# One added product with 64 stationary columns, in the seven-product pairs and in the channel products of a two-layer trunk kernel

## The chip, the cores and the metric

The kernel runs on one core of one Trainium2 chip. The metric is the device time of one execution in microseconds. Three runs of the kernel before are given, and one more execution was profiled.

## The reference

Two layers, each with four phases that add to the residual `h` (512 tokens of 1024 values): a feed-forward half step, a mixer of three head groups, a cross attention to 256 memory tokens, and a second feed-forward half step. The feed-forward, which takes most of the time, is

```python
def swiglu_ffn(x, w_up, w_down):
    gate, up = jnp.split(x @ w_up, 2, axis=-1)
    return (jax.nn.silu(gate) * up) @ w_down
...
    h = h + 0.5 * rms_norm(ff, g[FFN1_POST])
```

with `x` 512 x 1024, `w_up` 1024 x 5632 and `w_down` 2816 x 1024, in float32. It occurs four times (two layers, two half steps).

## The kernel before

**Parts of a product.** Every weight and every activation is split in two parts, hi and lo (`whi`, `wlo`, `xhi`, `xlo`), and a product of the reference is three products on TensorE (hi hi, hi lo, lo hi), each of the type fp32r. ScalarE makes the hi part of a weight, VectorE the lo part, from the raw weights (`wraw`) that SP's queue loads.

**The upward product.** The input's transposed form lies in `xhi`, `xlo` as eight blocks of 128 channels by 512 tokens. The first channel blocks of a phase are done by `chans`, in two halves of 256 tokens: for the first `nj` outputs (4) a bank of PSUM is held, the first half of the tokens is multiplied for all of them, then the second half; that lets the work begin when two of the four token tiles are normalised. Further outputs take all 512 tokens at once. A product of `chans` writes a tile `ch`. The transposes that bring the next token tiles in (`tp<-ident,xn`, four to a group) stand between the products of `chans`.

**Seven products.** From the fourth pair of hidden blocks on (`SEVEN = range(3, NF)`, 19 pairs to an upward stretch, two outputs of 128 to a pair) an output block is made by seven products of half size instead of eight (`products`). They use sums of input blocks made once a phase (`form`) and sums of weight blocks made for each pair (`sums`). In the trace they write tiles `p`. Each of the seven is 4 channel blocks times 3 parts, so 12 TensorE products with 128 stationary columns and 256 moving ones, and a pair is 84. The seven run in the order P1 (weights `a`), P6 (`c`), P2 (`d`), P7 (`c`), P5 (`b`), P3 (`b`), P4 (`a`). VectorE joins their results (`w`), ScalarE applies the silu (`sg`).

**Order.** The streams (loads, splits, products, normalisation) are generators; a modelled clock picks the one that can start first and so fixes the order in which each engine's instructions are written. Nothing is reordered on the chip except by what waits.

Of the kernel before, what the change touches and what calls it, by code (L numbers as in the profile page):

```python
# [69 lines left out]
SEVEN = range(3, NF)  # L70
# [196 lines left out]
class Weave:  # L267
# [455 lines left out]
    def chans(self, n, nj, sink, over=None):  # L723

        held = []
        for half in range(2):
            for t in range(2):
                yield ("x", self.phase, 2 * half + t)
            for i in range(nj):
                if not half:  # L730
                    yield {"cur": 1}
                    held.append(self.bank("ch", True))
                    u = yield from self.unit(self.n(i))
                u = self.u[self.n(i)]
                yield from self.chan(held[i], u, 256 * half, 256 * half + 256, i == 0)
                if half:
                    self.spent(self.n(i))
                    sink(i, held[i])
        for i in range(nj, n):
            if self.n(i) in self.seven:  # L740
                yield from self.products(i)
            if self.n(i) in self.seven or self.n(i - 1) in self.seven:
                continue
            u = yield from self.unit(self.n(i))
            yield {"cur": 1}
            ps = self.bank("ch", True)
            yield from self.chan(ps, u, 0, S)
            self.spent(self.n(i))
            sink(i, ps)
        if over is not None:  # L750
            over()

    def products(self, i):

        k = self.k
        f, i = i // 2, self.n(i)
        yield ("forms",)

        def x(kh, th):
            return tuple(q[:, 4 * kh:4 * kh + 4, 256 * th:256 * th + 256] for q in (k.xhi, k.xlo))

        def prod(out, u, h, x, first=True, last=True):
            for kk in range(4):
                if kk % 2 == 0:
                    yield "T"
                k.mm3(out, tuple(q[:, 4 * h:4 * h + 4] for q in u), kk, (x[0][:, kk], x[1][:, kk]), first and kk == 0, last and kk == 3)

        lo, hi = slice(0, 256), slice(256, 512)  # L770
        s1, s2, s3, s4 = self.sx

        def bank(name):
            ps = self.bank(name, True)
            banks[name] = ps
            return ps

        banks = {}
        a = yield from self.unit((i, "a"))
        yield {"cur": 1}  # L780
        ps = bank("p17")
        self.spawn(self.combine(f, banks), 2 * f)
        yield from prod(ps[:, lo], a, 0, x(0, 0))
        self.fire(("P1", f))
        c = yield from self.unit((i, "c"))
        yield {"cur": 1}
        p2 = bank("p62")
        yield from prod(p2[:, lo], c, 1, s2)
        self.given(f, 2, 3)
        d = yield from self.unit((i, "d"))  # L790
        yield from prod(p2[:, hi], d, 0, x(1, 0))
        self.fire(("P2", f))
        self.spent((i, "d"))
        yield from prod(ps[:, hi], c, 0, s3)
        self.fire(("P7", f))
        self.given(f, 4, 5)
        self.spent((i, "c"))
        b = yield from self.unit((i, "b"))
        yield {"cur": 1}
        yield from prod(bank("p5")[:, lo], b, 0, s1)  # L800
        self.given(f, 0, 1)
        self.fire(("p5", f))
        yield {"cur": 1}
        ps = bank("p34")
        yield from prod(ps[:, hi], b, 1, x(1, 1))
        self.spent((i, "b"))
        yield from prod(ps[:, lo], a, 1, s4)
        self.fire(("p4", f))
        self.spent((i, "a"))
        if f == SEVEN[-1]:  # L810
            self.fire(("sevens",))

    def given(self, f, *tiles):

        if f == SEVEN[-1]:
            tiles = [j for j in tiles if self.phase or j < 4]
            self.hs_free.extend(tiles)
            self.free(hs=len(tiles))
# [1595 lines left out]
```

## Time and profile before

| | |
|---|---|
| three runs | 2329.0, 2330.9, 2335.39 us, median 2330.9 |
| the profiled execution | 2327.65 us, span of its instructions 2325.9 us |
| TensorE products | 15128, busy 99% of the span |
| VectorE / ScalarE / GpSimd busy | 79% / 50% / 12% |
| HBM | 138 GB/s over the span |

Products on TensorE are pipelined: the next one starts before the last has ended, so that the engine reads as busy throughout, and the time that one product costs is the distance from its start to the start of the next. That distance is called the pace below.

### The profile page before, as it was taken

The page shows a single profiled execution, that of the slowest core. Times are in us where ns is not written, and L with a number is a line of the kernel's source. Part 1 is how long each engine was busy: PE and PEld are TensorE (multiplying, and loading weights), DVE is VectorE, ACT ScalarE, POOL GpSimd, SP SyncE. Part 2 cuts the span into 40 slices and gives each one's busy share as a digit, 9 for nine tenths or more (in the row PEclk, how much of TensorE's full clock was granted, in tenths as well). Part 3 has the DMA queues.
Part 4 walks back from the last instruction along what each step waited for, and adds up shares of the span by engine and source line. Part 5 has one row for each costly group of instructions (what it writes and reads, how often), then busy time and mean ns, then how long its engine had stood idle before and what let it go on. Part 6 is the DMA issues. An engine that isn't in the chain of part 4 may idle for free.

```text
span 2325.9 us, 39137 instructions
## 1 busy us (share of the span) xinstructions
PE 2292.5 (99%) x15128; PEld 2066.8 (89%) x15128; DVE 1833.0 (79%) x2746; ACT 1155.4 (50%) x1963; POOL 290.0 (12%) x406
## 2 busy tenths in 40 slices
PE   9999999998999999999999999999999999999998
PEld 8999889887888899998899998897878888999987
DVE  7999777887766689996789996778876666999865
ACT  4444555544554454445544445545345545544554
POOL 2000011444200100000000000032442101000000
PEclk9999999999999999999999999999999999999999
DMA  5333676323555343336633336643236544333464
GB/s 166 105 105 110 218 218 179 89 71 93 192 207 181 110 127 109 106 112 192 180 110 109 109 112 197 194 107 95 61 121 210 182 166 133 103 108 110 126 200 145
DMA packets 323441, 323.72 MB, mean 139 GB/s; under 512 B 29507, under 2 KB 264501, under 8 KB 323254
## 3 DMA queue, kind: packets, MB, share of 16 engines
q1 hardware_dynamic: 323254, 321.21, 45.1%
q8 instruction: 119, 1.95, 0.3%
q14 instruction: 68, 0.56, 0.1%
HBM read 301.50 MB, written 19.66 MB: 138 GB/s over the span
## 4 chain that ended last, share of the span: by engine, by line
PE 92%; DVE 3%; ACT 2%; issue 1%; POOL 1%; DMA 0%; SPq 0%; DVEq 0%; POOLq 0%; ACTq 0%
PE p L141 32%; PE dn L141 27%; PE ch L141 14%; PE tk L141 4%; PE kv L141 4%; PE tp L141 1%; PE xs L141 1%; PE xo L141 1%; PE mo L141 1%; PE iy L141 1%; ACT whi L141 1%; PE iu L141 1%; POOL ss L141 1%; PE py L141 1%; PE mp L141 1%
## 5 line engine op out<-in xcount | busy, mean ns | idle before, releaser
L141 DVE TENSOR_TENSOR wlo<-wraw,whi 128x1024 fp32r<-128x1024 f32 (+2 forms) x491 | 564.1, 1149 | 180.6 <-ACT whi L141 179.8
L141 ACT ACTIVATE whi<-wraw 128x1024 fp32r<-128x1024 f32 (+2 forms) x492 | 481.8, 980 | 223.8 <-PE dn L141 134.3
L141 PE MATMUL p<-form,whi 128*128 128x256 f32 x2432 | 440.3, 281 | 0.0
L141 PE MATMUL dn<-whi,hs 128*128 128x512 f32 x1376 | 379.1, 391 | 0.0
L141 PEld LDWEIGHTS p<-form,whi 128*128 128x128 f32 x2432 | 376.2, 190 | 1.0
L141 PE MATMUL p<-form,wlo 128*128 128x256 f32 x1216 | 341.8, 281 | 0.0
L141 ACT ACTIVATE whi<-sums 128x1024 fp32r<-128x1024 f32 x152 | 161.2, 1063 | 309.8 <-DVE sums L141 223.8
L141 PEld LDWEIGHTS dn<-whi,hs 128*128 128x128 f32 x1376 | 255.4, 188 | 50.9
L141 PE MATMUL p<-xhi,whi 128*128 128x256 f32 x912 | 256.3, 281 | 0.0
L141 PE MATMUL p<-xhi,wlo 128*128 128x256 f32 x912 | 256.3, 281 | 0.0
L141 PE MATMUL p<-xlo,whi 128*128 128x256 f32 x912 | 256.3, 281 | 0.0
L141 PEld LDWEIGHTS p<-form,wlo 128*128 128x128 f32 x1216 | 228.3, 188 | 0.0
L141 PE MATMUL ch<-xhi,whi 128*128 128x256 f32 (+1 forms) x688 | 217.6, 323 | 0.2
L141 DVE TENSOR_TENSOR wlo<-sums,whi 128x1024 fp32r<-128x1024 f32 x152 | 185.0, 1219 | 38.5 <-ACT whi L141 38.5
L141 PE MATMUL dn<-wlo,hs 128*128 128x512 f32 x688 | 214.3, 390 | 0.0
L141 PE MATMUL ch<-xhi,wlo 128*128 128x256 f32 (+1 forms) x688 | 214.0, 318 | 0.2
L141 POOL TENSOR_SCALAR ss<-ss 128x1 f32<-128x1 f32 (+1 forms) x80 | 41.3, 516 | 1369.9 <-ACT jk L141 1232.5
L141 PE MATMUL ch<-xlo,whi 128*128 128x256 f32 (+1 forms) x688 | 202.2, 317 | 0.0
L141 DVE TENSOR_TENSOR w<-p,w 128x512 f32<-128x512 f32 (+1 forms) x304 | 187.3, 616 | 5.7 <-PE p L141 5.6
L141 PEld LDWEIGHTS p<-xlo,whi 128*128 128x128 f32 x912 | 175.1, 192 | 0.4
L141 PEld LDWEIGHTS p<-xhi,whi 128*128 128x128 f32 x912 | 171.2, 188 | 0.5
L141 PEld LDWEIGHTS p<-xhi,wlo 128*128 128x128 f32 x912 | 171.2, 188 | 0.0
(373 smaller groups left out, 4182.3 us busy)
## 6 DMA issues: line engine op xcount, KB each, us to landing
wraw<-in_ffn_w_down_dram SPq DMA_DIRECT2D x172, 512.0 KB
wraw<-in_ffn_w_up_dram SPq DMA_DIRECT2D x304, 256.0 KB
wraw<-in_w_in_dram SPq DMA_DIRECT2D x32, 512.0 KB
wraw<-in_xa_w_kv_dram SPq DMA_DIRECT2D x32, 512.0 KB
wraw<-in_w_out_dram SPq DMA_DIRECT2D x30, 512.0 KB
wraw<-in_xa_w_o_dram SPq DMA_DIRECT2D x30, 512.0 KB
wraw<-in_ffn_w_up_dram SPq DMA_DIRECT2D x24, 512.0 KB
xkv<-kvs SPq DMA_DIRECT2D x32, 256.0 KB
```

The lines of the kernel that those rows point to most:

```text
L141: return f(*args, **kw)
```

## The change

A method `pace` issues one TensorE product with 64 stationary columns (half of the 128) and 256 moving ones, into the first 64 partitions of a bank that the next product overwrites. It is called in two places: in `products`, in the first pair of each upward stretch only, between P1 and P6; and in `chans`, before the second output (`i == 1`) of the first token half. Nothing is removed.

```diff
@@ chans
                     u = yield from self.unit(self.n(i))
+                    if i == 1:
+                        yield "T"
+                        self.pace(held[i], u)
                 u = self.u[self.n(i)]
...
@@ products
         p2 = bank("p62")
+        if f == SEVEN[0]:
+            yield "T"
+            self.pace(p2, c)
         yield from prod(p2[:, lo], c, 1, s2)
...
+    def pace(self, ps, w):
+
+
+        self.T.matmul(ps[:64, :256], w[0][:, 0, :64], self.k.xhi[:, 0, :256], start=True, stop=True)
```

TensorE's order around the first pair of the first upward stretch, in the changed kernel (a row is a product, output tile, moving and stationary operand, partitions by moving columns; `p_653` is the bank of P1, `p_672` that of P6 and P2):

```order
256 L141 MATMUL p_653<-xhi,whi 128x256
257 L141 MATMUL p_653<-xlo,whi 128x256
258 L141 MATMUL p_653<-xhi,wlo 128x256
259 L141 MATMUL p_672<-xhi,whi 64x256
260 L141 MATMUL p_672<-form,whi 128x256 x2
261 L141 MATMUL p_672<-form,wlo 128x256
262 L141 MATMUL p_672<-form,whi 128x256 x2
```

One row came in, between the 12 products of P1 and the 12 of P6; there are four such rows in the program, one for each upward stretch.

TensorE's order in the last phase of the first layer (second feed-forward), at the end of the first output of `chans`, changed kernel first, where `tp` is a group of four transposes:

```order
3350 L141 MATMUL ch<-xlo,whi 128x256 x4
3351 L141 MATMUL ch<-xhi,whi 64x256
3352 L141 MATMUL ch<-xhi,whi 128x256
3353 L141 MATMUL ch<-xlo,whi 128x256
3354 L141 MATMUL ch<-xhi,wlo 128x256
3355 L141 MATMUL ch<-xhi,whi 128x256
3356 L141 MATMUL ch<-xlo,whi 128x256
3357 L141 MATMUL ch<-xhi,wlo 128x256
3358 L141 MATMUL tp<-ident,xn 128x128 x4
```

And the same place before:

```order
3350 L141 MATMUL ch<-xhi,wlo 128x256
3351 L141 MATMUL ch<-xhi,whi 128x256
3352 L141 MATMUL ch<-xlo,whi 128x256
3353 L141 MATMUL ch<-xhi,wlo 128x256
3354 L141 MATMUL ch<-xhi,whi 128x256
3355 L141 MATMUL ch<-xlo,whi 128x256
3356 L141 MATMUL ch<-xhi,wlo 128x256
3357 L141 MATMUL tp<-ident,xn 128x128 x4
```

The added product stands behind the first output's 24 products, and the modelled clock now writes the first group of transposes 6 products earlier: 30 products of `chans` stand ahead of it instead of 36. There are eight such added rows, one for each phase, and a group of transposes moves 6 products forward in five of the phases.

## Rows read from the trace of the kernel before

**Rows 1.** The page: busy time by engine; costliest groups (busy us, mean ns).
```profile
PE 2292.5 (99%) x15128; PEld 2066.8 (89%) x15128; DVE 1833.0 (79%) x2746; ACT 1155.4 (50%) x1963; POOL 290.0 (12%) x406
...
L141 PE MATMUL p<-form,whi 128*128 128x256 f32 x2432 | 440.3, 281 | 0.0
```

**Rows 2.** Windows: busy us (count) by engine, granted clock, DMA share, GB/s.
```profile
52.48:236.80 184.32, 184.32 (x1566) 184.31 (x1565) 171.23 (x224) 83.62 (x114) 0.00 (x0) 1.00 0.37 107
...
2011.52:2195.73 184.21, 184.21 (x1566) 184.21 (x1564) 171.41 (x223) 83.82 (x115) 0.00 (x0) 1.00 0.37 108
...
1989.85:2000.50 10.65, 10.65 (x95) 10.65 (x95) 10.55 (x11) 6.73 (x8) 0.00 (x0) 1.00 0.18 51
```

**Rows 3.** Timeline, PE, where the first upward stretch begins: start us, us.
```profile
52.26 0.39 PE L141 MATMUL ch<-xhi,wlo 128*128 128x512 f32 x1
52.48 0.28 PE L141 MATMUL p<-xhi,whi 128*128 128x256 f32 x1
...
53.19 0.28 PE L141 MATMUL p<-xhi,whi 128*128 128x256 f32 x1
```

**Rows 4.** Timeline, PE, products with 64 stationary columns within the mixer.
```profile
562.44 0.28 PE L141 MATMUL kv<-wraw,wlo 128*128 128x256 f32 x1
562.64 0.43 PE L141 MATMUL mo<-pair,gt 128*64 128x128 f32 x2
563.01 0.50 PE L141 MATMUL kv<-wraw,whi 128*128 128x256 f32 x2
563.35 0.28 PE L141 MATMUL kv<-wraw,wlo 128*128 128x256 f32 x1
```

**Rows 5.** Timeline, PE, behind four products of 64 rows by 64 columns.
```profile
611.49 0.41 PE L141 MATMUL it<-ident,pair 64*64 64x64 f32 x4
...
612.52 0.28 PE L141 MATMUL kv<-mch,wlo 128*128 128x256 f32 x1
...
613.20 0.28 PE L141 MATMUL kv<-mch,wlo 128*128 128x256 f32 x1
```

**Rows 6.** Timeline, PE, behind a wait in the channel products of a later phase.
```profile
838.86 0.28 PE L141 MATMUL ch<-xhi,whi 128*128 128x256 f32 x1
...
839.21 0.28 PE L141 MATMUL ch<-xhi,wlo 128*128 128x256 f32 x1
```

**Rows 7.** Timeline, PE, behind one product with 114 stationary rows and moving columns.
```profile
27.33 0.26 PE L141 MATMUL psp<-ident,prow 114*128 114x114 f32 x1
...
27.56 0.28 PE L141 MATMUL ch<-xlo,whi 128*128 128x256 f32 x1
...
28.15 0.28 PE L141 MATMUL ch<-xhi,whi 128*128 128x256 f32 x1
```

**Rows 8.** Timeline, PE, the attention scores `xs` behind a fast channel stretch.
```profile
727.26 1.11 PE L141 MATMUL xs<-xkT,xq 128*128 128x256 f32 x8
```

**Rows 9.** Timeline, DVE, one pair of an upward stretch; idle time before in brackets.
```profile
101.72 1.22 DVE L141 TENSOR_TENSOR wlo<-sums,whi 128x1024 fp32r<-128x1024 f32 x1 [0.48 <-ACT whi L141]
...
103.46 0.68 DVE L141 TENSOR_TENSOR wlo<-wraw,whi 128x512 fp32r<-128x512 f32 x1
104.30 0.69 DVE L141 TENSOR_TENSOR hid<-w,sg 128x512 f32<-128x512 f32 x1 [0.16 <-ACT sg L141]
...
111.61 1.23 DVE L141 TENSOR_TENSOR wlo<-sums,whi 128x1024 fp32r<-128x1024 f32 x1 [0.48 <-ACT whi L141]
```

**Rows 10.** Timeline, ACT and PE, the same pair.
```profile
100.62 1.06 ACT L141 ACTIVATE whi<-sums 128x1024 fp32r<-128x1024 f32 x1 [0.90 <-PE p L141]
...
105.02 0.28 PE L141 MATMUL p<-xhi,wlo 128*128 128x256 f32 x1
```

**Rows 11.** Timeline, PE, first transposes of two phases, idle time before in brackets.
```profile
829.49 0.63 PE L141 MATMUL tp<-ident,xn 128*128 128x128 f32 x4 [1.25 <-DVE xn L141]
...
1175.15 0.63 PE L141 MATMUL tp<-ident,xn 128*128 128x128 f32 x4 [0.20 <-DVE xn L141]
```

## The prediction

> **What bounds the kernel now.** I read the page first, then windows over the four upward stretches, then the timeline of TensorE product by product, and last VectorE's and ScalarE's timeline for one pair. The page has TensorE busy for 99% of the span and VectorE for 79% [rows 1]. A busy TensorE says little, since its products overlap, so the question is how far apart they start. In an upward stretch it is issued without a hole: the window from the first `p` product's start at 52.48 to the last one's at 236.80 counts 1566 products, one of which is the product still running at its start, so 1565 steps in 184.32 us, 117.8 ns a step; the fourth stretch has 184.21 us for the same count, and the two between lie with it [rows 2]. The granted clock is 1.00 there, the 2.4 GHz level. VectorE is busy for 171.2 of the 184.3 us, 93%.
>
> The same kind of product (128 stationary columns, 256 moving) also runs faster here. In the channel products of the last phase, at the same granted clock, 94 steps take 10.65 us, 113.3 ns each [rows 2]. So there are **two paces**, 113.3 and 117.8 ns, 4.44 ns or 3.8% apart, and next to nothing between them for long. In the whole trace all 6384 `p` products run at the slow one; the page gives their mean duration as 281 ns [rows 1].
>
> What selects the pace? Sorting all starts of 256-column streams by what stands ahead of them gives this. Behind products with 512 moving columns the stream is always slow; the upward stretch begins so, at 52.48, right behind a `ch` product of 512, and six steps later (53.19) stands at 118 ns a step [rows 3]. Behind 64-column or 64-row products, or a wait, where TensorE has first run empty, 13 of 15 streams come out fast. After the two `mo` products with 64 columns, the next two steps are long (0.34 us from 563.01 to 563.35) [rows 4] and by the fifth the stream is fast; behind the 64 x 64 products of `it` the six steps from 612.52 to 613.20 take 0.68 us, 113 ns each [rows 5]. All six streams directly behind `mo` end so. The two exceptions stand behind a wait (the three steps from 838.86 take 0.35 us, 117 ns [rows 6], and it stays so for 94 products) and behind a 64-row product. One narrower product without running empty does the reverse: behind the 114-row `psp`, the five steps from 27.56 to 28.15 are 118 ns [rows 7], where the stream was fast up to it.
>
> **The change, part by part.**
>
> *The pace.* The added product of an upward stretch stands behind the 12 products of P1. 1566 - 12 = 1554 products of each stretch follow without another stationary shape or moving length between them. If the stream comes out fast, it saves 4 x 1554 x 4.44 ns = **27.6 us**; if not, 0. I take the upper end: in the rows a drain by a 64-column product is what most nearly precedes a fast stream, and the slow pace's own trigger (512 columns) does not occur again until the stretch ends. Loads of stationary columns that wait for a semaphore stand in fast channel stretches too, two to an output, and don't end them.
>
> *Will VectorE follow?* A pair is 84 products: 9.89 us slow, 9.52 us fast. VectorE's cycle shows two holes a pair, 0.48 and 0.16 us, and repeats after 111.61 - 101.72 = 9.89 us [rows 9], so its work is 9.25 us. The 0.48 us hole stands behind a ScalarE split that itself waited 0.90 us for TensorE to give up the old stationary buffer [rows 10]; it shrinks when TensorE is faster. With the 0.16 us left, VectorE needs 9.41 us, 0.11 us less than 9.52. The closest delivery is weights `d`: VectorE ends its split at 103.46 + 0.68 = 104.14 [rows 9] and TensorE first reads it at 105.02 [rows 10], 0.88 us of lead, of which some 38 faster products between the release and the read take 0.17 us. So TensorE remains the bound, with little to spare. Should VectorE bound at 9.7 us instead, half of the gain goes.
>
> *The product itself.* No 64-column fp32r product of 256 columns is in the trace. From `mo`: 0.20 us from the last full product to the first 64-column one (562.44 to 562.64), 0.37 for the two of them (562.64 to 563.01), of which I take the way back out as 0.20 too, and 0.34 us for the next two steps, 0.22 and 0.12 [rows 4]. Put into a slow stream, that is 0.20 + 0.20 + 0.22 us in place of two steps of 0.118, **0.39 us more** per product. Below, it is bounded by one step of 0.11 us. The nearest rows show the full drain, so I take 0.39. In the four upward stretches nothing hides it: 4 x 0.39 = 1.6 us.
>
> *The eight in `chans`.* In six phases TensorE waits for VectorE's `xn` at the transposes that follow; the two first waits shown are 1.25 and 0.20 us beyond the last product's end [rows 11]. The drain lies in these waits, so it is paid in two phases, 0.8 us; without the cover it would be 8 x 0.39 = 3.1 us. The 6 or 12 products between it and the transposes gain at most 12 x 4.44 ns, 0.05 us a phase; I take 0.2 us together.
>
> *The moved transposes.* In five phases a group of transposes stands 6 products earlier. Where it waits for `xn` anyway, the wait grows by 6 x 0.113 = 0.68 us, and these six products follow later. What they fill there is a later wait (the next transposes, the second token half), so a part returns. Bounds 0 and 5 x 0.68 = 3.4 us; I take 1.5, near the middle, since two of the five have such a later wait in full and the others only a small one. DMA issues don't move by more than these steps.
>
> *Sum*, against the profiled execution: 2327.65 - 27.6 + 1.6 + 0.8 - 0.2 + 1.5 = 2303.8 us. That execution lies 3.25 us under the median of the three runs, 2330.9, and under all of them; on the median's scale the sum is 2330.9 - 23.9 = 2307. I give **2306**.
>
> [...]
>
> **Rivals.**
>
> *A. The added product doesn't change the pace.* For it: no `p` product was ever fast, `form` is never a moving operand in a fast stream, a narrower one has set the slow pace [rows 7], and two of 15 drained streams came out slow [rows 6]. Against it: the six behind `mo`, and the `xhi` halves of P2 and P3 are the operands of the fast channel stretches. What is left are the costs, 1.6 + 0.8 + 1.5 = 3.9 us: 2334.8 on the median's scale, no change.
>
> *B. The fast pace holds only in part.* Something in a pair drops it, or VectorE binds. The drop exists: at 727.26 the `xs` products, whose stationary loads wait one behind the other, take over from a fast stream, and the eight end after 1.11 us, so seven steps of 0.83 / 7 = 118 ns [rows 8]. Against it: in a pair such loads stand two products apart, as in the fast channel stretches. Half of 27.6 is 13.8 us: 2306 + 13.8 = 2320.
>
> *C. Slower.* The pace stays slow and the drains of `chans`, with the moved transposes behind them, are all in the open, as they would be if `xn` came later by the same amount: 12 x 0.39 + 3.4 = 8.1 us, 2339. It decides from 7 us on. Against it: the waits of 1.25 us that the first transposes have now [rows 11].
>
> **How the numbers follow.** All four stretches fast: 0.70, with its own range 2300 to 2312 (the drains at 0.11 us and no loss at the transposes below; 3.4 us and all drains in the open above). B 0.11, A 0.14, C 0.05. The first and B make 0.81, so the range reaches from 2298 to 2326 (one stretch of 6.9 us being fast less than half lies at its end). About 0.3%, 7 us, is what a measurement of this kernel can tell from no change: the three runs span 6.4 us. Faster by more: the first case and most of B, 0.78. Within: A and the rest, 0.17. Slower: 0.05.
>
> **What would show it.** Right: windows over the upward stretches of 177.5 us where they were 184.3, with the same products; steps of 113 ns from the fifth product behind the added one on; 0.20 us on either side of it; VectorE's hole of 0.48 us reduced to about 0.1. Wrong: steps of 118 ns behind the added product, or a window that begins at 113 and goes back; a pair that takes longer than 9.52 us with TensorE's loads waiting for VectorE's `wlo`; or transposes that wait for more than 0.7 us longer than before.

## The result, and the profile after

The changed kernel takes 2304.64 us (median of four runs, 2302.91 to 2308.49), the kernel before 2330.56 us beside it on the same chip (2329.0 to 2335.39). The ratio is 0.9888, with a 95% interval from 0.9868 to 0.9907, so the change gains 25.9 us or 1.1%. The profiled execution took 2305.66 us, with a span of 2303.9 us; that of before had 2327.65 and 2325.9, so the two traces are 22.0 us apart.

The page of the changed kernel has the engines within a point of their shares in [rows 1], and a mean duration of `p` products of 276 ns in place of 281:

```profile
PE 2267.6 (98%) x15140; PEld 2041.8 (89%) x15140; DVE 1833.6 (80%) x2746; ACT 1155.7 (50%) x1963; POOL 292.7 (13%) x406
...
L141 PE MATMUL p<-form,whi 128*128 128x256 f32 x2432 | 425.4, 276 | 0.0
```

The busy shares, 98% and 99%, don't show the gain. The windows over the upward stretches do (columns as in [rows 2], from the first `p` product to the first `dn`, the downward product, behind them; the lower two begin 0.06 us behind that first product):

```profile
52.55:230.22 177.67, 177.67 (x1569) 177.67 (x1567) 171.19 (x224) 83.67 (x114) 0.00 (x0) 1.00 0.38 111
858.41:1036.02 177.61, 177.61 (x1568) 177.61 (x1567) 171.59 (x224) 84.02 (x114) 0.00 (x0) 1.00 0.38 112
...
1996.40:2174.01 177.61, 177.61 (x1569) 177.61 (x1567) 171.14 (x224) 83.62 (x114) 0.00 (x0) 1.00 0.38 111
```

From the first `p` to the first `dn` it was 184.44 us before, and it is 177.67 us now: **6.77 us less in each of the four stretches, 27.1 us together**, with one product more in each. The granted clock is 1.00 as before, so this isn't the clock. VectorE does the same 171 us of work in the shorter window and is busy for 96% of it.

TensorE's timeline shows the place where the pace turns (start us, us):

```profile
53.61 0.28 PE L141 MATMUL p<-xhi,whi 128*128 128x256 f32 x1
53.73 0.28 PE L141 MATMUL p<-xlo,whi 128*128 128x256 f32 x1
53.84 0.28 PE L141 MATMUL p<-xhi,wlo 128*128 128x256 f32 x1
53.96 0.28 PE L141 MATMUL p<-xhi,whi 128*64 128x256 f32 x1
54.08 0.40 PE L141 MATMUL p<-form,whi 128*128 128x256 f32 x2
54.32 0.28 PE L141 MATMUL p<-form,wlo 128*128 128x256 f32 x1
54.44 0.39 PE L141 MATMUL p<-form,whi 128*128 128x256 f32 x2
54.66 0.28 PE L141 MATMUL p<-form,wlo 128*128 128x256 f32 x1
```

The 64-column product starts one ordinary step behind its predecessor (0.12 us) and the next one starts an ordinary step behind it. The two products from 54.08 still take 0.24 us, the two from 54.44 take 0.22. From there on the stream keeps its pace to the end of the stretch: of its 1566 steps between `p` products 1551 are of 113 or 114 ns, and between 60 and 135 us they average 113.33 ns, where they averaged 117.78 before.

VectorE's cycle in one pair, which answers to [rows 9]:

```profile
98.84 2.54 DVE L141 TENSOR_TENSOR wlo<-sums,whi 128x1024 fp32r<-128x1024 f32 x2
...
102.74 0.69 DVE L141 TENSOR_TENSOR hid<-w,sg 128x512 f32<-128x512 f32 x1 [0.16 <-ACT sg L141]
...
108.36 1.22 DVE L141 TENSOR_TENSOR wlo<-sums,whi 128x1024 fp32r<-128x1024 f32 x1
```

It repeats after 108.36 - 98.84 = 9.52 us, where it was 9.89. The hole of 0.48 us between the two `wlo` of `sums` has nearly closed: the two are now one group of 2.54 us for two instructions of 1.22, so at most 0.1 us lies between them. Ahead of it ScalarE waits 0.51 us for TensorE instead of 0.90 [rows 10]:

```profile
99.06 1.06 ACT L141 ACTIVATE whi<-sums 128x1024 fp32r<-128x1024 f32 x1 [0.51 <-PE p L141]
```

Of the 27.1 us, the traces keep 22.0. In the stretches of channel products 4.5 us are lost. The most is lost in the second feed-forward of the first layer (1.89 us), where TensorE waits 1.85 us for the transposes' operand instead of 1.25 [rows 11], and where in this execution the clock was halved just behind it. The rows are of the timeline and of windows:

```profile
825.13 0.81 PE L141 MATMUL tp<-ident,xn 128*128 128x128 f32 x4 [1.85 <-DVE xn L141]
...
826.59 0.41 PE L141 MATMUL ch<-xlo,whi 128*128 128x256 f32 x1
826.80 0.41 PE L141 MATMUL ch<-xhi,wlo 128*128 128x256 f32 x1
```
```profile
825.40:828.80 3.40, 3.40 (x19) 3.40 (x18) 3.40 (x5) 2.77 (x6) 0.00 (x0) 0.51 0.47 137
```

Steps of 0.21 us at a granted clock of 0.51, the 1.2 GHz level: at the 0.113 us of the other level those 3.4 us would have taken about half. The other 0.6 us or so lie in the mixers and elsewhere (+1.4 us in the first mixer, -1.1 in the second).

### The profile page after: what moved, and what is told of

It is laid out like the page before. It is cut to its first block, busy times and chain, and to the rows that moved or that the text cites. A ratio compares the mean times of both kernels' runs of the same rounds, so it can differ in the third digit from the quotient of the medians.

```text
span 2303.9 us, 39161 instructions
## 1 busy us (share of the span) xinstructions
PE 2267.6 (98%) x15140; PEld 2041.8 (89%) x15140; DVE 1833.6 (80%) x2746; ACT 1155.7 (50%) x1963; POOL 292.7 (13%) x406
## 4 chain that ended last, share of the span: by engine, by line
PE 91%; DVE 3%; ACT 3%; POOL 1%; issue 1%; DMA 0%; SPq 0%; DVEq 0%; POOLq 0%; ACTq 0%
PE p L141 31%; PE dn L141 26%; PE ch L141 13%; PE tk L141 4%; PE kv L141 4%; PE tp L141 1%; PE xs L141 1%; PE xo L141 1%; POOL ss L141 1%; ACT whi L141 1%; PE mo L141 1%; PE iy L141 1%; PE iu L141 1%; PE py L141 1%; PE mp L141 1%
## 5 line engine op out<-in xcount | busy, mean ns | idle before, releaser
L141 PE MATMUL p<-form,whi 128*128 128x256 f32 x2432 | 425.4, 276 | 0.0
L141 PEld LDWEIGHTS p<-form,whi 128*128 128x128 f32 x2432 | 366.9, 188 | 1.0
L141 PE MATMUL p<-form,wlo 128*128 128x256 f32 x1216 | 335.8, 276 | 0.0
L141 PE MATMUL ch<-xhi,whi 128*128 128x256 f32 (+2 forms) x696 | 219.5, 324 | 0.5 <-ACT xhi L141 0.5
```

Of the source, the lines that this page charges most:

```text
L141: return f(*args, **kw)
```

## The experiments

The theory to begin with: the added product turns a stream that runs at 117.8 ns a step into one of 113.3 ns, in the pairs alone, and nothing else in the change gains. The rivals were that the gain is in the channel products or in the order that they move, or that any added product does it.

**The pairs alone, the channels alone, a full product, the order kept.** Four kernels on one chip. The first two have one of the change's two calls each. The third has the call in the pairs, with all 128 columns:

```diff
-        self.T.matmul(ps[:64, :256], w[0][:, 0, :64], self.k.xhi[:, 0, :256], start=True, stop=True)
+        self.T.matmul(ps[:, :256], w[0][:, 0], self.k.xhi[:, 0, :256], start=True, stop=True)
```

The fourth has both calls, but issues the product without telling the modelled clock, so that every other instruction stands where it stood before:

```diff
-                        yield "T"
                         self.pace(held[i], u)
...
-        self.T.matmul(ps[:64, :256], w[0][:, 0, :64], self.k.xhi[:, 0, :256], start=True, stop=True)
+        self.T.eng.matmul(ps[:64, :256], w[0][:, 0, :64], self.k.xhi[:, 0, :256], start=True, stop=True)
```

> The four products in the seven-product pairs alone, none in the channel products. Theory 1 (the 64-column product turns the stream behind it fast at once, and what the change loses between the upward stretches comes from the eight in the channel products and the transposes that they move forward): each upward stretch 6.8 us shorter as in the changed kernel, the channel products as before, so 27 us below the kernel before, about 2303.5 us, and some 4 to 5 us below the changed kernel in the profile's own stretches. Theory 2 (the loss between the stretches comes of something else, such as a stretch that begins earlier against its loads): no better than the changed kernel, 22 to 26 us below the kernel before.

> The eight products in the channel products alone, none in the pairs. Theory 1: the upward stretches stay at 117.8 ns a product and the channel products lose what they lost in the changed kernel, about 4 us: 2334 to 2336 us. Theory 2: the channel products as before, 2330.6 us within 1 us.

> As the first of these, but the added product of the pairs has 128 stationary columns, no half. Theory 1: the half width is what turns the pace, so nothing changes but four products of 0.12 us: 2331 us, steps of 117.8 ns throughout. Rival (any product more, or a changed place of the boundaries between banks, turns it): fast as with 64 columns, 2303.5 us.

> All twelve products as in the change, but issued past the modelled clock and without a scheduling step of their own, so that every engine's order is that of the kernel before with twelve products put in. Theory 1 with the moved transposes as the loss: 27 us below the kernel before less 2 to 12 times 0.12 us, about 2304 us, and the first transposes wait no longer than before. Rival (the products in the channel stretches cost by themselves, not by the order): as the changed kernel, 4 to 5 us above the run with the pairs alone.

Beside the kernel before at 2329.27 us:

| | median, us | ratio, 95% interval | each upward stretch |
|---|---|---|---|
| pairs alone | 2303.92 | 0.9885, 0.9871 to 0.9898 | -6.77 us |
| channels alone | 2332.23 | 1.0006, 0.9998 to 1.0015 | 0.00 us |
| full width, pairs | 2329.56 (ten runs, one of them 8028.04, which the ratio leaves out) | 0.9998, 0.9988 to 1.0007 | +0.12 us |
| both, order kept | 2303.81 | 0.9882, 0.9867 to 0.9897 | -6.77 us |

The whole gain is that of the four products in the pairs: the order kept does no worse, so the moved order isn't what gains. With the order kept the first transposes of the second feed-forward wait 1.16 us, against 1.25 before and 1.85 in the change. An equal product of full width costs its own step and changes nothing: in its timeline the steps stay at 0.12 us, 0.23 to 0.24 for two.

```profile
54.00 0.28 PE L141 MATMUL p<-xhi,whi 128*128 128x256 f32 x1
54.12 0.28 PE L141 MATMUL p<-xlo,whi 128*128 128x256 f32 x1
...
54.47 0.40 PE L141 MATMUL p<-form,whi 128*128 128x256 f32 x2
54.70 0.28 PE L141 MATMUL p<-form,wlo 128*128 128x256 f32 x1
54.82 0.40 PE L141 MATMUL p<-form,whi 128*128 128x256 f32 x2
```

The channels alone lie between what its two theories gave, 2334 to 2336 us and 2330.6; with them the first upward stretch is as slow as ever, 184.44 us at a clock of 1.00:

```profile
52.13:236.57 184.44, 184.44 (x1567) 184.44 (x1566) 170.11 (x222) 83.58 (x113) 0.00 (x0) 1.00 0.37 107
```

**Where it is put, and what undoes it.** If the pace is a state that a product sets and that lasts, the same product nine pairs later must gain from there on alone, and a product of 512 moving columns must end the gain.

```diff
-        if f == SEVEN[0]:
+        if f == SEVEN[9]:
             yield "T"
             self.pace(p2, c)
```
```diff
+        if f == SEVEN[9]:
+            yield "T"
+            self.T.matmul(p2, c[0][:, 0], self.k.xhi[:, 0, :512], start=True, stop=True)
```

The first has the product in the tenth pair alone. The second keeps it in the first pair, and in the tenth adds a product of 512 moving columns into the bank that the next product overwrites.

> The 64-column product in the tenth pair of each upward stretch in place of the first. Theory 1 (one product turns the stream from there on, and nothing in a pair turns it back): 768 products at 117.8 ns, then 798 at 113.3 ns, each stretch 3.4 us shorter than before, 2316 us in all. Rival (the first pair of a stretch is what mattered, for instance VectorE's lead there): 2330 us, or all of the gain.

> The 64-column product in the first pair, and in the tenth pair one product with 128 stationary and 512 moving columns at the same place. Theory 1 with 512 moving columns as what sets the slow pace: fast for 756 products, slow from there on, each stretch 3.0 us shorter than before, 2317.5 us. Rival (once fast, only a change of stage ends it; the slow pace behind 512 columns in the kernel before came of something else at the start of a stretch): fast throughout, 2304.5 us.

Both stand beside the kernel before at 2330.42 us on their chip. The tenth pair alone: 2316.58 us, ratio 0.9944 (0.9929 to 0.9959), each stretch 3.41 us shorter. The 512: 2318.95 us, ratio 0.9951 (0.9934 to 0.9967), each stretch 3.00 us shorter. In the windows of the first, cut at the added product, the two paces stand side by side (770 and 801 products in the same time, each count with the one or two still running at its start):

```profile
52.00:142.46 90.46, 90.46 (x770) 90.45 (x768) 84.03 (x109) 40.31 (x54) 0.00 (x0) 1.00 0.37 107
142.46:233.03 90.57, 90.57 (x801) 90.57 (x800) 87.40 (x116) 43.55 (x60) 0.00 (x0) 1.00 0.38 112
```

The timeline of the second shows how the pace is lost:

```profile
139.21 0.28 PE L141 MATMUL p<-xlo,whi 128*128 128x256 f32 x1
139.32 0.28 PE L141 MATMUL p<-xhi,wlo 128*128 128x256 f32 x1
139.44 0.39 PE L141 MATMUL p<-xhi,whi 128*128 128x512 f32 x1
139.66 0.40 PE L141 MATMUL p<-form,whi 128*128 128x256 f32 x2
139.90 0.28 PE L141 MATMUL p<-form,wlo 128*128 128x256 f32 x1
140.02 0.40 PE L141 MATMUL p<-form,whi 128*128 128x256 f32 x2
140.25 0.28 PE L141 MATMUL p<-form,wlo 128*128 128x256 f32 x1
```

The steps ahead are 113 ns; the 512 takes 226 ns; the next pairs of products take 0.24 and 0.23 us. Between 145 and 229 us the steps average 117.78 ns again. All four stretches do the same. So the pace is a lasting state, and the prediction's reading that 512 columns set the slow one [rows 3] is shown by a run that adds nothing else to the pairs alone.

**What about the product turns it?** The prediction took it from places where TensorE had run empty. Two kernels have other odd products at the same place: 128 stationary by 128 moving columns, and 96 stationary by 256.

```diff
-        self.T.matmul(ps[:64, :256], w[0][:, 0, :64], self.k.xhi[:, 0, :256], start=True, stop=True)
+        self.T.matmul(ps[:, :128], w[0][:, 0], self.k.xhi[:, 0, :128], start=True, stop=True)
...
+        self.T.matmul(ps[:96, :256], w[0][:, 0, :96], self.k.xhi[:, 0, :256], start=True, stop=True)
```

> In the first pair, in place of the 64-column product, one with 128 stationary and 128 moving columns. Theory 1a (what turns the pace is a shorter load of stationary columns): slow throughout, 2330 us. Rival 1b (any product whose length breaks the regular step turns it): fast, 2304 us.

> In the first pair, in place of the 64-column product, one with 96 stationary columns. Theory 1a (a shorter load of stationary columns, by any amount that exceeds the 4.4 ns between the paces): fast, 2304 us. Rival 1c (the half width, for which the array takes another column setting, is what counts): slow, 2330 us.

Both gain as much: 2302.78 us, ratio 0.9883 (0.9863 to 0.9903), 6.77 us a stretch for 128 moving columns; 2303.71 us, 0.9887 (0.9867 to 0.9907), 6.79 us for 96 stationary ones. The timeline with 128 moving columns:

```profile
53.64 0.28 PE L141 MATMUL p<-xhi,wlo 128*128 128x256 f32 x1
53.76 0.22 PE L141 MATMUL p<-xhi,whi 128*128 128x128 f32 x1
53.82 0.45 PE L141 MATMUL p<-form,whi 128*128 128x256 f32 x2
54.11 0.28 PE L141 MATMUL p<-form,wlo 128*128 128x256 f32 x1
...
54.58 0.39 PE L141 MATMUL p<-form,whi 128*128 128x256 f32 x2
```

And with 96 stationary columns:

```profile
54.10 0.28 PE L141 MATMUL p<-xhi,wlo 128*128 128x256 f32 x1
54.23 0.28 PE L141 MATMUL p<-xhi,whi 128*96 128x256 f32 x1
54.34 0.39 PE L141 MATMUL p<-form,whi 128*128 128x256 f32 x2
54.57 0.28 PE L141 MATMUL p<-form,wlo 128*128 128x256 f32 x1
```

The short product starts 0.06 us ahead of its successor, the next steps are long, and the fast pace follows; behind 96 columns it is there almost at once (the first two steps behind it take 0.23 us, the next 0.11). In neither has TensorE run empty. A theory that wants a shorter load of stationary columns falls with the first, one that wants exactly half of them with the second. What is left is an odd product whose load or stream is shorter than the others'. Whether a mere pause between two full products would do as well, no run tried.

It is not a rule for any odd product. The narrow `psp` still sets the slow pace in the first phase of these two traces and of the others, as in [rows 7], and no run here took it apart. The added products of the change turned the slow stream in the seven later channel stretches of each trace, but in the first phase, where the product stands two products behind a group of transposes, two executions of the same kernel differ. Seven steps behind it take 0.80 us in the change's first trace, 114 ns each, and 0.82 us in its second (from the last set below), 117 ns each:

```profile
21.94 0.28 PE L141 MATMUL ch<-xlo,whi 128*128 128x256 f32 x1
...
22.74 0.28 PE L141 MATMUL ch<-xhi,wlo 128*128 128x256 f32 x1
```
```profile
21.54 0.28 PE L141 MATMUL ch<-xlo,whi 128*128 128x256 f32 x1
...
22.36 0.28 PE L141 MATMUL ch<-xhi,wlo 128*128 128x256 f32 x1
```

Nor do the products ahead decide the pace behind a wait. The stream of [rows 6] has the same products of its phase ahead of it, in the same order, in the kernel before and in the full-width run, and the same 93 steps take 10.95 us in the one and 10.54 in the other, both at a clock of 1.00:

```profile
838.86:849.81 10.95, 10.95 (x96) 10.95 (x94) 10.85 (x12) 7.03 (x9) 0.00 (x0) 1.00 0.30 99
```
```profile
839.00:849.54 10.54, 10.54 (x95) 10.54 (x94) 10.44 (x11) 6.62 (x8) 0.00 (x0) 1.00 0.27 89
```

So what is shown for the added product is a turn inside a settled slow stream; what a stream starts with behind transposes or a wait varies from execution to execution.

**What the channel products cost, and a version of both.** Once more the change, the pairs alone, and a third kernel in which all instructions keep the order of before and a 96-column product stands in the first pair and in both token halves of every channel stretch (20 in all), with the kernel before at 2329.76 us on the same chip.

```diff
+                if i == 1:
+                    self.pace(held[i], u, 256 * half)
...
+        self.T.eng.matmul(ps[:96, c0:c0 + 256], w[0][:, 0, :96], self.k.xhi[:, 0, :256], start=True, stop=True)
```

> The change once more, beside the next run on one chip, to measure what the eight products among the channel products cost by their moved transposes. Theory: in the change's profiled execution the four channel stretches were 4.3 us longer than before's, in the run without those products 0.5 us longer, so the change is to come out 1 to 4 us above the next run. Rival: these were differences of single executions, set by where the spells of half clock fell, and the two medians differ by less than 1 us.

> The four products in the up stretches alone, none among the channel products. Theory: about 2303.5 us, 1 to 4 us below the change on the same chip, each up stretch again 6.77 us shorter than before's. Rival: within 1 us of the change.

> All instructions in the order of the kernel before; a product with 96 of its columns in each up stretch's first pair and in both token halves of each of the eight channel stretches, 20 products in all. Theory: each half stretch of channel products that by chance ran at 117.8 ns a step gains its 0.4 us and each added product costs 0.1 us, so it ends within 1.5 us of the run with the four products alone, below it if anything, and 1 to 4 us below the change. Rival: sixteen more products cost 2 us or more together and it ends above the run with four.

| | median (range of four runs), us | ratio, 95% interval | span of the trace |
|---|---|---|---|
| the change | 2303.97 (2302.1 to 2305.68) | 0.9889, 0.9874 to 0.9904 | 2303.6 |
| pairs alone | 2303.03 (2301.77 to 2304.26) | 0.9884, 0.9867 to 0.9900 | 2302.3 |
| 20 products | 2305.55 (2301.83 to 2309.31) | 0.9896, 0.9879 to 0.9913 | 2301.5 |

In time the three are not told apart: 0.94 us between the first two is within the spread, as the rival had it, and the third lies 2.5 us above the second, not within the 1.5 us expected, with four runs that span 7.5 us. The traces do show the cost at its place. The first transposes of the second feed-forward, the change first and the pairs alone second:

```profile
824.89 0.63 PE L141 MATMUL tp<-ident,xn 128*128 128x128 f32 x4 [1.85 <-DVE xn L141]
```
```profile
823.50 0.63 PE L141 MATMUL tp<-ident,xn 128*128 128x128 f32 x4 [1.26 <-DVE xn L141]
```

Six products fewer stand ahead of that wait, and it is 0.59 us longer, and the six follow behind it: this stretch is 0.67 us longer in the change, the six steps of 113 ns (0.68 us). The second mixer loses its part another way. Its first group of transposes hasn't moved, but two later groups now stand together, eight in a row, and the stream behind them is slow in all three traces with that order (the change's two and the channels alone), fast in the other ten: its last 100 steps take 11.78 us in the change and 11.34 in the pairs alone.

```profile
1514.42:1526.20 11.78, 11.78 (x103) 11.78 (x101) 8.98 (x13) 3.65 (x4) 0.00 (x0) 1.00 0.16 33
```
```profile
1512.38:1523.72 11.34, 11.34 (x102) 11.34 (x101) 8.76 (x13) 4.16 (x5) 0.00 (x0) 1.00 0.14 31
```

Over the eight stretches the differences are 0.02, 0.81, -0.11, 0.67, -0.01, 0.44, -0.11 and 0.67, together 2.4 us. The spans are only 1.3 us apart, because other stretches of the same instructions differ by as much with the opposite sign (-1.8 us in the second mixer). The 20 products change nothing in sum: their eight channel stretches are 0.1 us shorter than those of the pairs alone. No version is shown to beat the change; the pairs alone do the same with four products.

## Why the prediction was right

**The pace** (27.6 us from 4 x 1554 steps of 4.44 ns): right. The steps are 113.33 ns over the whole stretch, the average had been 117.78. It rested on a choice of which rows come nearest, the `mo` rows [rows 4] against `psp` [rows 7], and the choice held. The reason behind it, that the stream turns where TensorE "has first run empty", did not: the full timelines above have no such place. Among the rows without a drain, where the added product turned out to belong, the prediction had `psp` alone, and that one said slow. So the forecast of the pace was right in part by luck. Its sorting of what stands ahead of a stream also has no class for those directly behind transposes that TensorE reached without a wait, and the exception that it named [rows 6] was a matter of the execution, as the full-width run shows.

**Will VectorE follow:** right in size. 9.52 us a pair, the hole of 0.48 us down to 0.1 or less, the one of 0.16 still there.

**The product itself** (0.39 us each, 1.6 us): the mis-sized step. The row that it came from shows a drain on either side of `mo` [rows 4]; the added product has none. 1554 x 4.44 ns is 6.90 us and the stretches gained 6.77, so one product costs 0.13 us, about one step, 0.5 us for four in place of 1.6. The lower bound that the prediction named, 0.11 us, was the nearly right end.

**The eight in the channels:** no drain is seen there either, so the 0.8 us is not there: what is left is a step of about 0.12 us each. The small gain (0.2 us) is not shown: the 0.11 us of each cross attention comes of a stream of 28 products that was slow in the pairs alone, and the first cross attention takes 21.69 us before and 21.80 in the change's first trace.

**The moved transposes** (1.5 us, between 0 and 3.4): 2.6 us in the four stretches that lengthened. The step that failed is "so a part returns": in the two second feed-forwards the whole 0.67 us stays: the six products fill no later wait. In the first mixer (0.81 us) TensorE now waits ahead of two groups of transposes that it reached without a wait before. The 0.44 us of the second mixer is no wait but a slow stream, a term that the prediction didn't have. The total is inside the bounds.

**The sum:** by the trace of the second set, 27.1 - 2.4 = 24.7 us, against 23.9 predicted (27.6 - 1.6 - 0.8 + 0.2 - 1.5). The two mis-sized terms offset each other in part. The medians give 25.9 us, the two profiled executions 22.0; that of before lay under all its runs and that of the change 1.0 us above its median, which makes the 3.9 us between the two numbers.

**A formula for one product.** The Trainium skill ("TensorE: Matmul & The Clock Gate", Back-to-back issue gap) has a formula, N / 2.4 + 2.5, for the gap of an isolated product with N moving columns, and says that in a stream of weight loads and products both set the spacing; for 256 columns an estimate by the formula is 109 ns. The steps measured here are of such a stream, and they are 113.33 or 117.78 ns, neither of them 109.

One more full-width product leaves the time at 2329.56 us, and with 64 of its columns it is 2303.92, 25.6 us less. So the distance between two products does not follow from their moving length alone.

**The rivals.** A falls: `form` is a moving operand in a fast stream now, in all 19 pairs up to the first `dn` product. B falls: no step goes back once the pace is fast, and VectorE keeps up with 6 us to spare in the stretch. C would have wanted the pace to stay slow; the channels alone take 2332.23 us beside 2329.27, which is not told from no change.

## What to carry to other kernels

Read the pace of a long run of equal products from start to start, not from busy shares: here two paces 3.8% apart stood in one trace at one clock, and one odd product set which of them each of the four long streams had. One product with a shorter load or a shorter stream behind the last 512-column one gave the fast pace for some 1550 products at the price of one step. Try it at the head of each long stream, measure it there, and see that it leaves the order of the other instructions alone: in the channel products the same edit moved transposes and gave back 2.4 us of trace, and with the order kept nothing of that is seen.

## What the runs showed of the hardware

The two paces are exact and stable. 113.33 ns is 272.0 periods of 2.4 GHz for 256 columns, the average over 660 steps of the change and over 740 of the tenth-pair run alike, and the slow pace is 117.78 ns, 282.7 periods, before the change and behind the 512-column product alike. A 512-column product in the fast stream takes 226 ns, twice the fast step, and still leaves the slow pace behind it. What holds the slow pace up, why an odd product of one kind ends it, and what decides the pace behind transposes, no run here shows.

The halved clock falls at other places in other executions. In the trace of the pairs alone and of the order kept, windows in the first mixer (granted clock third from the end):

```profile
526.90:537.10 10.20, 7.45 (x25) 4.88 (x24) 7.98 (x14) 2.59 (x8) 6.61 (x7) 0.50 0.43 101
...
578.10:581.50 3.40, 3.35 (x14) 2.82 (x14) 1.54 (x6) 1.32 (x4) 1.58 (x2) 0.50 0.76 293
```
```profile
527.70:537.90 10.20, 6.91 (x17) 4.26 (x18) 7.98 (x14) 2.59 (x8) 6.64 (x8) 0.50 0.40 97
...
578.90:589.10 10.20, 10.20 (x42) 8.48 (x40) 5.53 (x15) 2.12 (x8) 2.35 (x3) 0.50 0.27 102
```

The second has 6.8 us more at the halved clock, and this mixer is 3.5 us longer in it, about half of those 6.8, with the instructions of the mixer unchanged. So single traces of this kernel differ by some us for a reason that is no part of any edit, and a stretch has to be compared at its own place, as the upward ones were.
